# Norm chains of a decoder layer's front end rearranged, and the dense experts' partial sums carried through PSUM by ScalarE

## The chip, the cores and the metric

The kernel runs on one core of one Trainium2 chip. The metric is the device time of one launch in microseconds; each figure given as "the time" is the median of several runs.

## The reference, cut to what matters

One decoder layer on 1024 tokens of width 1024, all in f32. The parts that the change touches:

```python
h = rms_norm(x, norm1_gain) * (1 + scale1) + shift1
r_q, r_k, r_v, r_g, s_q, s_k, s_v = split(h @ w_in)            # 8 heads of 64 in each
y_ret = head_group_norm(retention(r_q, r_k, r_v)) * silu(r_g)  # mean and variance over 64
q_sb, k_sb = rms_norm(s_q, sb_q_gain), rms_norm(s_k, sb_k_gain)    # per head, over 64
z = q_sb @ k_sb.T / 8                                          # stick-breaking attention
log_beta = log_sigmoid(z)
...
x = x + gate1 * (concat(y_ret, rms_norm(y_sb)) @ w_out)
h2 = rms_norm(x, norm2_gain) * (1 + scale2) + shift2
# PEER: 8 heads, top 16 of 128 x 128 product keys, 16384 experts of one neuron each
a = gelu(h2 . expert_down[id]) * gate
x = x + gate2 * sum(a * expert_up[id])
```

## The kernel before

The 1024 tokens are eight tiles of 128. The attention part, which we call the front end, runs in three segments of 1, 3 and 4 tiles (`SEGS`). In each segment the seven projections are streams: eight 256 KB pieces of `w_in` come in, ScalarE and GpSimd split each piece into a high and a low half, and TensorE accumulates three products for each tile in an `acc` bank of PSUM. When a stream ends, an `ev_...` function evicts each tile's bank: `ev_rk`, `ev_rq`, `ev_rv`, `ev_rg` for retention, `ev_sk`, `ev_sq`, `ev_sv` for stick-breaking. The order of the last three streams and of the retention work between them is the string `RET` (h = `ret_head`, t = `ret_tail`).

Four norms form chains that cross engines. `head_norm` (L390, for `ev_sk` and `ev_sq`) squares the bank on ScalarE, sums over the head on VectorE, calls `rpow` (L79: scale and add epsilon on VectorE, power of -1/2 on GpSimd) and multiplies the bank by the result on VectorE (L396); then TensorE transposes the product (L327). `normed` (L299) does the same over the whole row before the transposes of L310. `ret_head` takes the mean off (L461, L463), squares, sums, calls `rpow` and multiplies (L470) before another transpose of L327. `sb_finish` (L542) takes sums of squares from TensorE in PSUM, adds epsilon on VectorE (L549), takes the power on GpSimd (L550), and copies on ScalarE before the transposes of L556. The stick-breaking weights are sigmoids of z and -z that ScalarE reads from PSUM (L514, L515); VectorE multiplies them up in a scan (L516).

The experts are computed in two ways. For tokens 0 to 511 (`gather_tile`) GpSimd issues one indirect DMA of 128 rows for each of 128 choices, once in `expert_down` and once in `expert_up`, for four tiles: 1024 gathers of 512 KB, each used up by one VectorE instruction (L780, L790). Four buffers `g` are in flight. Gathers 480 to 495 wait for the fifth piece of the dense part's routing (`HOLD`, `HOLD_C`), and all behind them on the queue with them. For tokens 512 to 1023 (`dense`) every expert is multiplied: stage 1 (L821 to L823) gives a block of 128 experts' activations, stage 2 (L924 to L926) adds the block's part to the output. Stage 2 goes in 32 groups of `GB` = 4 blocks; in each group it has eight output pieces of 128x512, numbered k. Pieces 0 and 1 stay in PSUM all the time (`held`). Pieces 2 to 7 take turns in the two other `acc` banks: twelve matmuls, and then VectorE adds the bank to `yacc` in SBUF (L937), or ScalarE copies it there in the first group (L935). In the last group (L930) VectorE multiplies by gate2 and adds.

The code is written in this order, the gathers last. The order of instructions on each engine is fixed at build time by the framework, which runs the program through a cost model and gives each engine the oldest piece of work that is ready (`schedule_with_timeline_sim`). So gathers lie between all the rest on VectorE's and GpSimd's queues, and each engine then keeps to that order on the chip.

Of the kernel before, what the change touches and what calls it, by code (L numbers as in the profile page):

```python
# [54 lines left out]
def tile_kernel(ctx, tc, A, out):  # L55
# [20 lines left out]
    def bcast_dram(ap, parts, n, off=0):  # L76
        return bass.AP(tensor=ap.tensor, offset=ap.offset + off, ap=[[0, parts], [1, n]])

    def rpow(o, in_, mul):  # L79
        DVE.tensor_scalar(o, in_, mul, EPS, op0=OP.mult, op1=OP.add)  # L80
        POOL.tensor_tensor(o, o, mhalf[:, 0:o.shape[-1]], op=OP.pow)


# [146 lines left out]
    def seg_gen(phase, t0, nt, hooks):  # L230
# [67 lines left out]

        def normed(x):  # L299
            st = small(1)  # L300
            ACT.activation(V((128, D), BF16), x, AF.Square, accum_out=st)
            rpow(st, st, 1.0 / D)
            ACT.activation(x, x, AF.Copy, scale=st)

        def to_T(xs, scale, shift):
# [11 lines left out]
        def hv(a):  # L317
            return a.rearrange("p (h d) -> p h d", d=64)
# [68 lines left out]
        stream(A["w_in"], 1536, hT_, ev_rg, False)  # L387


        def head_norm(acc, o):  # L390
            sq = V()
            ACT.activation(sq, acc, AF.Square)
            s = small(8)
            DVE.tensor_reduce(s, hv(sq), axis=AX.X, op=OP.add)
            rpow(s, s, 1.0 / 64)
            DVE.tensor_tensor(hv(o), hv(acc), s[:, :, None].to_broadcast([128, 8, 64]), op=OP.mult)  # L396

        def ev_sk(i, acc):
            t = t0 + i
            kn = V()  # L400
            head_norm(acc, kn)
            tp = transpose4(kn, anti)
            ACT.activation(kTr[:, :, 896 - 128 * t:1024 - 128 * t], q4(tp), AF.Copy, scale=gqk)

        qc = [U([128, 2, 512]) for i in range((nt + 1) // 2)]
        qT = [qc[i // 2][:, i % 2] for i in range(nt)]

        def ev_sq(i, acc):
            qn = V()
            head_norm(acc, qn)  # L410
            copy(qT[i], transpose4(qn, ident))

        def ev_sv(i, acc):
            v = V()
# [6 lines left out]
        def ret_head(i):  # L421
# [36 lines left out]
                                                     op0=OP.mult, op1=OP.add)  # L458
            mu = small(8)
            DVE.tensor_reduce(mu, hv(y), axis=AX.X, op=OP.add)  # L460
            DVE.tensor_scalar(mu, mu, 1.0 / 64, None, op0=OP.mult)  # L461
            yc = V()
            DVE.tensor_tensor(hv(yc), hv(y), mu[:, :, None].to_broadcast([128, 8, 64]), op=OP.subtract)  # L463
            sq = V()
            ACT.activation(sq, yc, AF.Square)
            va = small(8)
            DVE.tensor_reduce(va, hv(sq), axis=AX.X, op=OP.add)
            rpow(va, va, 1.0 / 64)
            DVE.tensor_mul(rg[i], rg[i], yc)
            DVE.tensor_tensor(hv(rg[i]), hv(rg[i]), va[:, :, None].to_broadcast([128, 8, 64]), op=OP.mult)  # L470

# [28 lines left out]
        def sb_weights(i, pr):  # L500
            t = t0 + i
            L = 128 * (t + 1)
            c0 = 896 - 128 * t
            w2 = []
            for hh in range(2):
                b = slice(64 * hh, 64 * hh + 64)
                be, sy = U([128, D]), U([128, D])
                for s0 in range(0, L, 512):
                    w = min(512, L - s0)
                    z = pstile("acc", 4)  # L510
                    PE.matmul(z[:, :w], q4(qT[i])[b, pr], kTr[b, pr, c0 + s0:c0 + s0 + w], start=True, stop=s0 > 0)
                    if s0 == 0:
                        PE.matmul(z[:, :128], ident, negm, start=False, stop=True)
                    ACT.activation(be[:, s0:s0 + w], z[:, :w], AF.Sigmoid)  # L514
                    ACT.activation(sy[:, s0:s0 + w], z[:, :w], AF.Sigmoid, scale=-1.0)  # L515
                DVE.tensor_tensor_scan(sy[:, :L], sy[:, :L], sy[:, :L], 1.0, op0=OP.mult, op1=OP.bypass)  # L516
                DVE.tensor_mul(be[:, 1:L], be[:, 1:L], sy[:, :L - 1])
                w2.append(be)
            return w2
# [22 lines left out]
        def sb_finish(i, yT):  # L542
# [3 lines left out]
            for pr in range(4):  # L546
                PE.matmul(tp[:, 2 * pr:2 * pr + 2], sq[:, pr], ones_bd[:, 0:128:64], start=True, stop=True)
            r = small(8)
            DVE.tensor_scalar(r, tp[:, 0:8], 1.0, EPS, op0=OP.mult, op1=OP.add)  # L549
            POOL.tensor_tensor(r, r, mhalf, op=OP.pow)  # L550
            tp = pstile("tp", 2)
            rx = V()
            copy(hv(rx), r[:, :, None].to_broadcast([128, 8, 64]))
# [246 lines left out]
    def dense(Hhi, Hlo, dp, kpg, late):  # L800
# [83 lines left out]
        for g0 in range(0, NB, GB):  # L884
# [28 lines left out]
            def stage2(k, bs):  # L913
                i, hf = divmod(k, 2)
                sl = slice(128 * i, 128 * i + 128)
                ds_ = slice(512 * hf, 512 * hf + 512)
                keep = k < len(held)
                if k not in ys:
                    ys[k] = held[k] if keep else pstile("acc", 4)
                y = ys[k]  # L920
                st, sp = not keep or g0 == 0, not keep or g0 + GB == NB
                for b in bs:
                    phi, plo, uhi, ulo = blk[b]
                    PE.matmul(y, phi[:, sl], uhi[:, ds_], start=st and b == 0, stop=False)  # L924
                    PE.matmul(y, phi[:, sl], ulo[:, ds_], start=False, stop=False)  # L925
                    PE.matmul(y, plo[:, sl], uhi[:, ds_], start=False, stop=sp and b == GB - 1)  # L926
                if b < GB - 1:
                    return
                ya = yacc[:, i, ds_]
                if g0 + GB == NB:  # L930
                    DVE.tensor_mul(ya, y, g2[:, ds_])
                    DVE.tensor_add(x1[i][:, ds_], x1[i][:, ds_], ya)
                    SP.dma_start(out[(NG + i) * 128:(NG + i + 1) * 128, ds_], x1[i][:, ds_])
                elif not keep and g0 == 0:
                    copy(yacc[:, i, ds_], y)  # L935
                elif not keep:
                    DVE.tensor_add(yacc[:, i, ds_], yacc[:, i, ds_], y)  # L937

            if g0 + GB == NB:

# [90 lines left out]
```

## Time and profile before

| what | value |
|---|---|
| runs | 3194.1, 3207.25, 3212.17 us, median 3207.25 us |
| profiled execution | 3201.63 us, its span 3199.8 us |
| TensorE matmul busy | 2693.4 us (84%) |
| VectorE busy | 2631.3 us (82%) |
| GpSimd busy | 1918.6 us (60%) |
| ScalarE busy | 1076.0 us (34%) |
| DMA | 899.19 MB, mean 281 GB/s |
| mean granted TensorE clock | 0.909 of full speed |

The shares are means over stages with different limits. The front end lies before about 1440 us, the dense part's routing between 1440 and 1840 us, the groups of stage 2 after 1840 us. PE is TensorE's matmuls, PEld its weight loads, DVE is VectorE, ACT ScalarE, POOL GpSimd, SP the queue of plain DMAs.

### The profile page before, as it was taken

The numbers are of one execution on the slowest core, as the hardware profiler recorded it, in microseconds if no ns is written. First come the engines' busy times: TensorE is split into PE (matmuls) and PEld (weight loads), VectorE is DVE, ScalarE is ACT, GpSimd is POOL, SyncE is SP. The second block draws the span as 40 slices with busy tenths as digits, with TensorE's granted clock in tenths as the row PEclk, the third lists the DMA queues.
The fourth block names the chain that finished last, engine by engine and source line by source line (L and its number), as shares of the span: only waits on it lengthen the run. The fifth ranks groups of instructions, "written<-read, shape, count | busy, mean of one in ns | idle before, by whom it ended". The sixth has DMA issues, their size and how long they took to land.

```text
span 3199.8 us, 38483 instructions
## 1 busy us (share of the span) xinstructions
PE 2693.4 (84%) x12308; PEld 2079.8 (65%) x12308; DVE 2631.3 (82%) x4913; ACT 1076.0 (34%) x1871; POOL 1918.6 (60%) x1542
## 2 busy tenths in 40 slices
PE   6867867777967678696878998869999999999997
PEld 2454654576755345575767787657887887888785
DVE  2269788789987899789999778999778877888888
ACT  1122224244321345332666632322232332222231
POOL 1025874677777567652478756556666666666664
PEclk9978886888978688897999999989999999999999
DMA  8688886898788766852368898788899999999897
GB/s 316 241 291 280 297 280 219 297 345 295 242 283 287 247 203 217 308 202 70 119 233 316 315 318 313 265 282 306 312 321 330 340 333 317 330 343 333 315 313 267
DMA packets 337642, 899.19 MB, mean 281 GB/s; under 512 B 38296, under 2 KB 105880, under 8 KB 333344
## 3 DMA queue, kind: packets, MB, share of 16 engines
q0 software_dynamic: 147456, 536.94, 48.3%
q1 hardware_dynamic: 189984, 359.80, 32.7%
q8 instruction: 97, 1.59, 0.2%
q14 instruction: 105, 0.86, 0.1%
HBM read 846.24 MB, written 50.35 MB: 280 GB/s over the span
## 4 chain that ended last, share of the span: by engine, by line
DVE 27%; PE 21%; DMA 21%; issue 15%; POOL 12%; ACT 2%; SPq 1%; POOLq 0%; DVEq 0%; ACTq 0%
DMA g<-in_up_dram,ids 10%; POOL g L769 8%; DVE g L780 5%; DMA g<-in_down_dram,ids 4%; DVE gy L790 4%; PE tp L821 2%; PE tp L822 2%; PE tp L823 2%; PE acc L263 2%; DMA rawu<-in_up_dram 2%; DVE p L860 2%; PE acc L924 2%; PE acc L926 2%; PE acc L925 2%; DVE dlo L812 1%
## 5 line engine op out<-in xcount | busy, mean ns | idle before, releaser
L769 POOL DMA_INDIRECT g<-in_up_dram,ids x512 | 594.8, 1162 | 404.7 <-DVE gy L790 281.2
L769 POOL DMA_INDIRECT g<-in_down_dram,ids x512 | 536.4, 1048 | 470.2 <-DVE g L780 275.9
L790 DVE SCALAR_TENSOR_TENSOR gy<-g,a,gy 128x1024 f32<-128x1024 f32 x508 | 651.3, 1282 | 148.2 <-DMA g<-in_up_dram,ids 144.8
L780 DVE SCALAR_TENSOR_TENSOR g<-g,gy 128x1024 f32<-128x1024 f32 x512 | 617.9, 1213 | 134.1 <-DMA g<-in_down_dram,ids 132.2
L924 PE MATMUL acc<-u,p 128*128 128x512 f32 x1024 | 402.2, 398 | 39.9 <-DVE yacc L937 20.4
L821 PE MATMUL tp<-Thi,dhi 128*128 128x512 f32 x1024 | 406.6, 397 | 30.0 <-ACT dhi L71 18.4
L926 PE MATMUL acc<-u,p 128*128 128x512 f32 x1024 | 386.6, 395 | 20.9 <-DVE p L906 20.9
L823 PE MATMUL tp<-Thi,dlo 128*128 128x512 f32 x1024 | 403.5, 394 | 0.5 <-POOL dlo L812 0.4
L822 PE MATMUL tp<-Tlo,dhi 128*128 128x512 f32 x1024 | 403.8, 394 | 0.0
L925 PE MATMUL acc<-u,p 128*128 128x512 f32 x1024 | 402.8, 395 | 0.0
L812 POOL TENSOR_TENSOR u<-rawu,u 128x1024 fp32r<-128x1024 f32 x128 | 306.4, 2403 | 32.0 <-ACT u L71 30.0
L271 POOL TENSOR_TENSOR wlo<-wraw,whi 128x512 fp32r<-128x512 f32 x182 | 236.8, 1307 | 95.4 <-ACT whi L71 64.8
L924 PEld LDWEIGHTS acc<-u,p 128*128 128x128 f32 x1024 | 194.9, 190 | 94.5 <-DVE yacc L937 27.4
L821 PEld LDWEIGHTS tp<-Thi,dhi 128*128 128x128 f32 x1024 | 195.3, 191 | 73.3 <-ACT dhi L71 19.4
L926 PEld LDWEIGHTS acc<-u,p 128*128 128x128 f32 x1024 | 194.7, 191 | 65.0 <-DVE p L906 24.4
L71 ACT ACTIVATE whi<-wraw 128x512 fp32r<-128x512 f32 x208 | 130.3, 630 | 311.8 <-DMA wraw<-in_w_in_dram 105.7
L71 ACT ACTIVATE u<-rawu 128x1024 fp32r<-128x1024 f32 x128 | 133.0, 1056 | 298.8 <-DMA rawu<-in_up_dram 195.5
L71 ACT ACTIVATE dhi<-rawd 128x1024 fp32r<-128x1024 f32 x128 | 135.4, 1058 | 278.0 <-PE tp L822 268.5
L280 PE MATMUL acc<-wlo,Thi 128*128 128x512 f32 x504 | 212.5, 422 | 16.1 <-POOL wlo L271 15.6
L823 PEld LDWEIGHTS tp<-Thi,dlo 128*128 128x128 f32 x1024 | 194.5, 190 | 41.6 <-POOL dlo L812 1.4
L925 PEld LDWEIGHTS acc<-u,p 128*128 128x128 f32 x1024 | 195.5, 191 | 40.0
L822 PEld LDWEIGHTS tp<-Tlo,dhi 128*128 128x128 f32 x1024 | 195.0, 190 | 39.5
(271 smaller groups left out, 4998.6 us busy)
## 6 DMA issues: line engine op xcount, KB each, us to landing
rawd<-in_downT_dram SPq DMA_DIRECT2D x128, 512.0 KB
rawu<-in_up_dram SPq DMA_DIRECT2D x128, 512.0 KB
gd<-u SPq DMA_DIRECT2D x32, 1024.0 KB
gm<-gd SPq DMA_DIRECT2D x512, 64.0 KB
wraw<-in_w_in_dram SPq DMA_DIRECT2D x112, 256.0 KB
u<-in_ada_w_dram SPq DMA_DIRECT2D x46, 512.0 KB
wraw<-in_wq_dram SPq DMA_DIRECT2D x64, 256.0 KB
u<-in_w_in_dram SPq DMA_DIRECT2D x28, 512.0 KB
```

The costliest lines, as they stand in the source:

```text
L71: ACT.activation(out_, in_, AF.Copy, scale=scale)
L271: (POOL if kt else DVE).tensor_sub(lo, raw, hi.bitcast(F32))
L769: POOL.indirect_dma_start(out=g, out_offset=None, in_=A[src], in_offset=bass.IndirectOffsetOnAxis(ap=groups[j // m][0][:, j % m:j % m + 1] ...
L780: DVE.scalar_tensor_tensor(g, g, 1.0, hp, op0=OP.mult, op1=OP.mult, accum_out=a[:, j:j + 1])
L790: DVE.scalar_tensor_tensor(y, g, a[:, j:j + 1], y, op0=OP.mult, op1=OP.add)
L812: eng.tensor_sub(lo, raw, hi.bitcast(F32))
L821: PE.matmul(a, dhi[:, sl], Hhi[:, kt], start=kt == 0, stop=False)
L822: PE.matmul(a, dhi[:, sl], Hlo[:, kt], start=False, stop=False)
L823: PE.matmul(a, dlo[:, sl], Hhi[:, kt], start=False, stop=kt == KT - 1)
L924: PE.matmul(y, phi[:, sl], uhi[:, ds_], start=st and b == 0, stop=False)
L925: PE.matmul(y, phi[:, sl], ulo[:, ds_], start=False, stop=False)
L926: PE.matmul(y, plo[:, sl], uhi[:, ds_], start=False, stop=sp and b == GB - 1)
```

## The change

In the front end `rpow` loses its scale: the squares are scaled in ScalarE's own instruction, and epsilon is added on GpSimd. `ev_sk` and `ev_sq` first copy the bank to SBUF on ScalarE. `ev_sk` then normalises the copy. `ev_sq` transposes the copy as it is; the heads' factors go to a small tile `qs` (factor and its negative) that the two sigmoids take as a scale. In `ret_head` the division of the mean goes into the subtraction. `sb_finish` copies the sums out of PSUM on ScalarE.

In stage 2, for pieces 2 to 7 of groups 1 to 30, ScalarE copies `yacc` into the new bank before the first matmul, no matmul restarts the sum, and ScalarE copies the bank back to `yacc` after the last; VectorE's addition is gone.

```diff
-    def rpow(o, in_, mul):
-        DVE.tensor_scalar(o, in_, mul, EPS, op0=OP.mult, op1=OP.add)
+    def rpow(o, in_):
+        POOL.tensor_scalar(o, in_, EPS, None, op0=OP.add)
         POOL.tensor_tensor(o, o, mhalf[:, 0:o.shape[-1]], op=OP.pow)
...
-            ACT.activation(V((128, D), BF16), x, AF.Square, accum_out=st)
-            rpow(st, st, 1.0 / D)
+            ACT.activation(V((128, D), BF16), x, AF.Square, scale=1.0 / 32, accum_out=st)
+            rpow(st, st)
...
-        def head_norm(acc, o):
+        def head_scale(x, s):
             sq = V()
-            ACT.activation(sq, acc, AF.Square)
-            s = small(8)
+            ACT.activation(sq, x, AF.Square, scale=0.125)
             DVE.tensor_reduce(s, hv(sq), axis=AX.X, op=OP.add)
-            rpow(s, s, 1.0 / 64)
-            DVE.tensor_tensor(hv(o), hv(acc), s[:, :, None].to_broadcast([128, 8, 64]), op=OP.mult)
+            rpow(s, s)
         def ev_sk(i, acc):
             t = t0 + i
             kn = V()
-            head_norm(acc, kn)
+            copy(kn, acc)
+            s = small(8)
+            head_scale(kn, s)
+            DVE.tensor_tensor(hv(kn), hv(kn), s[:, :, None].to_broadcast([128, 8, 64]), op=OP.mult)
...
         def ev_sq(i, acc):
-            qn = V()
-            head_norm(acc, qn)
-            copy(qT[i], transpose4(qn, ident))
+            q = V()
+            copy(q, acc)
+            copy(qT[i], transpose4(q, ident))
+            head_scale(q, qs[i][:, 0])
+            DVE.tensor_scalar(qs[i][:, 1], qs[i][:, 0], -1.0, None, op0=OP.mult)
...
-            DVE.tensor_scalar(mu, mu, 1.0 / 64, None, op0=OP.mult)
             yc = V()
-            DVE.tensor_tensor(hv(yc), hv(y), mu[:, :, None].to_broadcast([128, 8, 64]), op=OP.subtract)
-            sq = V()
-            ACT.activation(sq, yc, AF.Square)
+            DVE.scalar_tensor_tensor(hv(yc), mu[:, :, None].to_broadcast([128, 8, 64]), -1.0 / 64, hv(y),
+                                     op0=OP.mult, op1=OP.add)
             va = small(8)
-            DVE.tensor_reduce(va, hv(sq), axis=AX.X, op=OP.add)
-            rpow(va, va, 1.0 / 64)
+            head_scale(yc, va)
...
-                    ACT.activation(be[:, s0:s0 + w], z[:, :w], AF.Sigmoid)
-                    ACT.activation(sy[:, s0:s0 + w], z[:, :w], AF.Sigmoid, scale=-1.0)
+                    h = 2 * pr + hh
+                    ACT.activation(be[:, s0:s0 + w], z[:, :w], AF.Sigmoid, scale=qs[i][:, 0, h:h + 1])
+                    ACT.activation(sy[:, s0:s0 + w], z[:, :w], AF.Sigmoid, scale=qs[i][:, 1, h:h + 1])
...
-            DVE.tensor_scalar(r, tp[:, 0:8], 1.0, EPS, op0=OP.mult, op1=OP.add)
-            POOL.tensor_tensor(r, r, mhalf, op=OP.pow)
+            copy(r, tp[:, 0:8])
+            rpow(r, r)
...
+                back = not keep and 0 < g0 < NB - GB
                 if k not in ys:
                     ys[k] = held[k] if keep else pstile("acc", 4)
+                    if back:
+                        copy(ys[k], yacc[:, i, ds_])
                 y = ys[k]
-                st, sp = not keep or g0 == 0, not keep or g0 + GB == NB
+                st, sp = not back and (not keep or g0 == 0), not keep or g0 + GB == NB
...
-                elif not keep and g0 == 0:
+                elif not keep:
                     copy(yacc[:, i, ds_], y)
-                elif not keep:
-                    DVE.tensor_add(yacc[:, i, ds_], yacc[:, i, ds_], y)
```

## Rows read from the trace of the kernel before

**Rows 1.** Windows: busy us of PE, PEld, DVE, ACT, POOL, clock, DMA share, GB/s

```profile
0.00:1440.00 1440.00, 1093.10 (x4979) 763.06 (x4980) 1131.42 (x2378) 468.62 (x894) 841.27 (x731) 0.84 0.79 269
...
1920.00:2160.00 240.00, 197.17 (x799) 155.77 (x798) 228.07 (x510) 65.69 (x84) 142.36 (x103) 0.90 0.84 286
2160.00:3184.00 1024.00, 1002.55 (x4370) 821.09 (x4368) 842.39 (x1028) 280.17 (x363) 652.09 (x488) 1.00 0.92 322
```

**Rows 2.** Windows of line 769, the gathers' issue on POOL

```profile
0.00:1440.00 1440.00, 537.55 (x480) 0.84 0.79 269
1440.00:1600.00 160.00, 0.00 (x0) 0.86 0.26 95
...
1920.00:3184.00 1264.00, 509.64 (x472) 0.98 0.90 315
```

**Rows 3.** Timeline from 3180 us: PE's last matmul, DVE's last gather product

```profile
3183.69 0.39 PE L926 MATMUL acc<-u,p 128*128 128x512 f32 x1
...
3190.64 1.29 DVE L790 SCALAR_TENSOR_TENSOR gy<-g,a,gy 128x1024 f32<-128x1024 f32 x1 [1.62 <-DMA g<-in_up_dram,ids]
```

**Rows 4.** Waits of PE in 0:1440: total us, times, longest

```profile
PE tp L327 <- DVE v L396: 77.4, 15, 17.0
PE tp L310 <- ACT u L303: 55.2, 15, 13.1
PE tp L556 <- ACT v L71: 39.0, 6, 10.4
PE tp L327 <- DVE u L470: 26.8, 2, 19.2
```

**Rows 5.** Timeline of PE: gaps before transposes, ident for Q, anti for K

```profile
103.83 1.08 PE L327 MATMUL tp<-ident,v 128*128 128x128 f32 x4 [3.39 <-DVE v L396]
...
448.92 1.09 PE L327 MATMUL tp<-ident,v 128*128 128x128 f32 x4 [17.00 <-DVE v L396]
...
927.79 2.04 PE L327 MATMUL tp<-anti,v 128*128 128x128 f32 x8 [14.46 <-DVE v L396]
...
990.99 1.11 PE L327 MATMUL tp<-ident,v 128*128 128x128 f32 x4 [12.02 <-DVE v L396]
...
1014.20 0.63 PE L327 MATMUL tp<-ident,v 128*128 128x128 f32 x4 [2.60 <-DVE v L396]
```

**Rows 6.** Timeline of DVE before the gap that ends at 990.99

```profile
983.23 0.16 DVE L80 TENSOR_SCALAR s<-s 128x8 f32<-128x8 f32 x1
983.30 1.22 DVE L780 SCALAR_TENSOR_TENSOR g<-g,gy 128x1024 f32<-128x1024 f32 x1
```

**Rows 7.** Groups by line and form: busy us, mean ns, then idle before

```profile
L81 POOL TENSOR_TENSOR s<-s,mhalf 128x8 f32<-128x8 f32 x24 | 40.1, 1671 | 47.3 <-DVE s L80 46.9
L71 ACT ACTIVATE gy<-g 128x1024 f32<-128x1024 f32 x4 | 4.1, 1024 | 1.3 <-DMA g<-h2d 1.3
L469 DVE TENSOR_TENSOR u<-u,v 128x512 f32<-128x512 f32 x8 | 6.8, 846 | 0.0
```

**Rows 8.** Groups of single tiles and lines: ns minimum/median/maximum, starts

```profile
L937 DVE TENSOR_TENSOR yacc<-yacc,acc x180: 661/681/692, 1912.9 to 3148.1; 128x512 f32<-128x512 f32 x180
L71 ACT ACTIVATE yacc<-acc x6: 592/598/598, 1872.2 to 1890.8; 128x512 f32<-128x512 f32 x6
L470 DVE TENSOR_TENSOR u<-u,s x8: 675/688/691, 89.7 to 1090.8; 128x512 f32<-128x512 f32 x8
```

**Rows 9.** Waits of PE in 1840:3184

```profile
PE acc L926 <- DVE p L906: 20.9, 7, 6.1
PE acc L924 <- DVE yacc L937: 20.4, 8, 5.4
PE acc L924 <- ACT p L71: 17.4, 13, 3.5
```

**Rows 10.** Waits of ACT in 1920:3184

```profile
ACT u L71 <- DMA rawu<-in_up_dram: 189.7, 49, 14.6
ACT p L71 <- DVE tp L903: 181.9, 55, 6.8
```

More of the change, by code (lines that the diff above doesn't have):

```diff
@@ L406, in seg_gen @@
         qT = [qc[i // 2][:, i % 2] for i in range(nt)]
+        qs = [vp.tile([128, 2, 8], F32, name="qs", bufs=4) for i in range(nt)]
         def ev_sq(i, acc):
-            qn = V()
-            head_norm(acc, qn)
-            copy(qT[i], transpose4(qn, ident))
+            q = V()
[3 more added lines that the diff above has]
+            DVE.tensor_scalar(qs[i][:, 1], qs[i][:, 0], -1.0, None, op0=OP.mult)
         def ev_sv(i, acc):
@@ L917, in stage2 @@
                 keep = k < len(held)
+                back = not keep and 0 < g0 < NB - GB
                 if k not in ys:
                     ys[k] = held[k] if keep else pstile("acc", 4)
+                    if back:
+                        copy(ys[k], yacc[:, i, ds_])
                 y = ys[k]
-                st, sp = not keep or g0 == 0, not keep or g0 + GB == NB
+                st, sp = not back and (not keep or g0 == 0), not keep or g0 + GB == NB
                 for b in bs:
                     phi, plo, uhi, ulo = blk[b]
-                    PE.matmul(y, phi[:, sl], uhi[:, ds_], start=st and b == 0, stop=False)
-                    PE.matmul(y, phi[:, sl], ulo[:, ds_], start=False, stop=False)
-                    PE.matmul(y, plo[:, sl], uhi[:, ds_], start=False, stop=sp and b == GB - 1)
+                    PE.matmul(y, phi[:, sl], uhi[:, ds_], start=st and b == 0, stop=False, skip_group_check=True)
+                    PE.matmul(y, phi[:, sl], ulo[:, ds_], start=False, stop=False, skip_group_check=True)
+                    PE.matmul(y, plo[:, sl], uhi[:, ds_], start=False, stop=sp and b == GB - 1, skip_group_check=True)
                 if b < GB - 1:
```

## The prediction

> **What bounds the kernel now.** I read the windows first, to part the stages, then in each stage what PE waits for, then the queues of the engines it waits for.
>
> The windows show two different kernels [rows 1]. Up to 1440 us no engine is full: PE is busy 1093 of 1440 us at a mean clock of 0.84, VectorE 1131, ScalarE 469, and the DMA engines 0.79 of the time. From 2160 us on PE is busy 1002.6 of 1024 us at full clock; that stage is bound by PE, with DMA close behind at 0.92. Between them, at 1920 to 2160, VectorE is busy 228 of 240 us and PE only 197: there the late routing of the gathered tokens loads VectorE.
>
> The gathers run beside all of this. 480 of them are issued by 1440 us, none from 1440 to 1600 us, since the next ones are held for the dense part's routing, and 472 in the last 1264 us, 2.68 us each [rows 2]. So the gathers have about 200 us in hand at the end of the front end, and a shorter front end moves the hold, and all behind it, forward by as much. At the end both halves finish together: PE's last matmul starts at 3183.7 us and VectorE's last gather product at 3190.6 us [rows 3]. To end earlier, both must.
>
> In the front end PE's largest waits are for the four norm chains: 77.4 us for L396 (Q and K), 55.2 us for `normed`, 39.0 us for `sb_finish`, 26.8 us for `ret_head` [rows 4], together 198 of PE's 347 idle us. In the dense part PE's waits are few: 20.4 us for the additions to be removed, 20.9 us for VectorE's low halves `plo`, 17.4 us for ScalarE's high halves `phi` [rows 9].
>
> **The change in the front end.** *Q.* Six gaps before a Q transpose make 42.5 us (3.39, 17.00, 12.02, 2.99, 4.49 and 2.60); the first, the two longest and the last stand in [rows 5]. The chain behind them is long because VectorE's short steps queue among gather products: a 0.16 us step is followed by one of 1.22 us [rows 6]. After the change a Q transpose waits for one ScalarE copy out of PSUM, 0.6 us by the same form [rows 8]. With handing over and ScalarE's queue I put 1.5 us on each of eight tiles: 42.5 - 12 is about 30 us saved. Bounds: 42.5 us, and nothing if PE only waits elsewhere. The chain itself goes on beside it and is wanted by the first sigmoid; the V stream (96 matmuls in the last segment) and the retention work lie between, longer than the 12 us it now costs. What comes late next on PE is the `ret_head` transpose.
>
> *K.* The other 77.4 - 42.5 = 35 us are K's. Its chain gets a ScalarE copy (0.6 us) longer and loses one VectorE place; the bank comes free after the copy, not after the product, so matmuls of the next stream may go first. Bounds: 35 us saved if they fill the gap, 8 x 1.5 = 12 us lost if not. I take 0, since the gap of 14.46 us [rows 5] is one chain long and the chain stays.
>
> *The other chains.* `normed`, `sb_finish` and `ret_head` each lose one VectorE place, `ret_head` two. A place is the step and one gather product before it, 0.16 + 1.22 = 1.4 us [rows 6]. About 15 such places end at a PE gap (5 of `normed`, 6 of `sb_finish`, 2 x 2 of `ret_head`): 21 us. GpSimd's added addition of 128x8 is in no row; it costs between nothing and the 1.67 us of the power of the same size [rows 7]. I take 0.5 us, since an addition is less than a power and both wait in one queue: -7 us. The `sb_finish` gaps lie beside VectorE's scans, which bound that stretch, so I count 10 us of the 14.
>
> The Trainium skill speaks against this step: "GPSIMD Engine Reference", section 3 on performance versus the Vector engine, keeps elementwise work on VectorE and gives a ratio of 1.96 for an addition. By that ratio, an estimate from the 0.16 us step, the addition would take 0.3 us, and the 15 places 5 us instead of 7.
>
> *At nothing:* the mean's division (8 x 0.16 us on VectorE), the 16 ScalarE copies and the scale operand of 192 sigmoids; ScalarE is busy 469 of 1440 us [rows 1]. Without that cover they would cost some 20 us. K's product now reads two SBUF operands; the nearest row, `ret_head`'s product from SBUF, takes 675 to 691 ns [rows 8], as the one from PSUM did.
>
> The Trainium skill's "SBUF — State Buffer", section "Who interferes with whom", has a VectorE instruction with two SBUF inputs contend with GpSimd instructions that read SBUF. The full-width product of L469 (846 ns mean, [rows 7]) may show that, the broadcast one of L470 doesn't; by the rule K's eight products would cost 1.3 us more. The removed additions have one PSUM input, so by it GpSimd gains nothing from their going.
>
> Front end together: 30 + 0 + 10 = 40 us saved. No DMA and nothing on SP's queue is added or moved.
>
> **The change in the dense part.** VectorE loses 180 x 0.681 = 123 us. ScalarE gains 180 copies out (0.598 us, [rows 8]) and 180 copies in; for a copy from SBUF to PSUM the row is 1.02 us at twice the width [rows 7], so 0.5 to 0.6 us. Together some 210 us over 1264, on an engine busy 346 there: 44%, not full.
>
> A bank's turnaround grows: before, one addition of 0.68 us; after, a copy out and a copy in, 1.2 us, before the next piece's first matmul. If all of the extra 0.5 us showed on PE, 180 x 0.5 = 92 us; if PE has matmuls of the other bank or of stage 1 to do, nothing. What decides is ScalarE's order. It waits 189.7 us for `rawu` from DMA (up to 14.6 us at a time) and 181.9 us for VectorE [rows 10]; a copy behind such a wait holds PE. The nearest row is PE's wait for `phi`, which stands in the same queue: 17.4 us [rows 9] for 128 copies, 0.14 us each, so 180 turnarounds cost about 25 us. Against it stand the 20.4 us of waits for L937 that go, and some of the 20.9 us for `plo`, which VectorE makes sooner. PE's idle time in 1920 to 3184 us is only 64 us in all (197.2 + 1002.6 busy of 1264, [rows 1]), so more can't be gained there. I take 0 for the sum, with bounds of -60 and +92.
>
> What freed VectorE time does start is gathers; at a DMA share of 0.92 they can gain only a few per cent, and need no more, since they only have to keep up with PE.
>
> **The sum.** The profiled execution took 3201.6 us; 3201.6 - 40 + 0 = 3161.6 us. The median of the runs is 5.6 us above it, so 3167 us.
>
> **The rivals.**
>
> *The dense part gains too.* VectorE's load of 228 in 240 us falls by its share of the 123 us, 23 us, PE's waits for it and what follows from it go, and the gathers keep up: two thirds of the 62 us of waits in [rows 9], 40 us more, 3127 us. For it: VectorE is full there. Against it: ScalarE waits for the same VectorE.
>
> *ScalarE holds PE (the slower side).* Its in-order waits for `rawu` and for VectorE fall before the copies in or out, and the turnaround's 0.5 us shows each time: 92 us, against 40 gained, 3259 us. It decides from 40/180 = 0.22 us for each turnaround. For it: the waits of [rows 10], longer than any slack of two banks. Against it: before, VectorE too waits for its gathers, and its additions held PE for 20.4 us only.
>
> *The front end gets no shorter.* The gaps only move to the next chain, since VectorE is busy 1131 of 1440 us and gathers fill what it gets free; dense part even: 3207 us. For it: the next chain, `ret_head`, is a 19.2 us gap right behind Q's. Against it: the Q gaps hold nothing on VectorE but gathers and other tiles' steps.
>
> **How the numbers follow.** The forecast has 0.52, its own range 3140 to 3190 (10 to 65 us saved); the dense gain 0.15; ScalarE's hold 0.18; no shorter front end 0.15. About 0.5%, 16 us, is what a measurement of this kernel can tell from no change. Faster: nearly all of the first, the second, a little of the last, 0.66. Same: most of the last and a weak form of the hold, 0.17. Slower: 0.17. The range goes from 3115, past the dense gain's 3127, to 3230, where the hold shows a little over 0.3 us for each turnaround; its full form lies outside.
>
> **What would show it.** Right: the gaps of 17.0 and 12.0 us before Q transposes fall under 2 us; the dense stage's first matmuls come about 40 us earlier; PE's wait at L924 for the copies in stays near 25 us, and PE stays 97% busy from then on. Wrong: PE waits at L924 for `acc` from ScalarE of over 65 us; or the K gaps grow; or the stage from 1920 us loses its idle time altogether.

## The result and the profile after

The changed kernel takes 3160.0 us (median of 3159.1, 3161.0, 3181.8 and 3140.8 us) against 3208.2 us (3194.1 to 3212.2 us, four runs), a ratio of 0.9874 with a 95% interval of 0.984 to 0.9908. It is faster by 1.3%, or 40 us. (The quotient of the two medians is 0.985, or 48 us; it lies in the interval as well.) The forecast was 3167 us, from a range of 3140 to 3190. The profiled execution took 3159.1 us with a span of 3157.3 us, 42.5 us under that of before, where the sum said 40.

The windows of the changed kernel, with the columns of [rows 1], show that both halves moved:

```profile
0.00:1440.00 1440.00, 1115.46 (x5128) 787.62 (x5128) 1146.26 (x2458) 504.79 (x935) 864.29 (x784) 0.86 0.80 271
...
1920.00:2160.00 240.00, 219.54 (x924) 176.74 (x923) 218.91 (x532) 116.41 (x174) 146.37 (x106) 0.96 0.88 303
2160.00:3140.00 980.00, 951.37 (x4130) 780.86 (x4129) 744.23 (x800) 410.80 (x610) 636.71 (x476) 0.99 0.92 325
```

PE is 97% busy in the last stretch (951.4 of 980 us), ScalarE 42% (before 27%), VectorE 76% (before 82%). At 1920 to 2160 us PE has 22 us more work in the same time than in [rows 1].

The waits of PE in the front end (0 to 1290 us: total us, times, longest), which answer to [rows 4]:

```profile
PE tp L310 <- ACT u L303: 48.4, 14, 12.3
PE tp L561 <- ACT v L71: 21.4, 7, 5.0
PE tp L327 <- DVE u L474: 20.6, 2, 16.3
...
PE tp L535 <- DVE u L522: 15.8, 7, 4.2
PE tp L446 <- DVE v L442: 13.2, 4, 10.1
...
PE tp L327 <- DVE v L403: 6.6, 5, 2.2
...
PE tp L327 <- ACT v L71: 1.8, 2, 1.1
```

`head_norm`'s 77.4 us have become 6.6 us for K (L403) and 1.8 us for Q's copy. `sb_finish` (now L561) fell from 39.0 to 21.4 us, `normed` from 55.2 to 48.4, `ret_head` (now L474) from 26.8 to 20.6. That makes 99.6 us of waits less, where the prediction counted 40. Some of it only moved: the waits at L535 and L446 were 0.9 and 4.7 us before (L530, L439). Up to the last score matmul (place A below) PE's idle time as a whole falls by 67 us, from 317.6 of 1268 to 250.8 of 1186 us. In PE's timeline the gaps before the transposes, which answer to [rows 5], are these (start, us, then the gap and its releaser):

```profile
906.92 1.13 PE L327 MATMUL tp<-anti,v 128*128 128x128 f32 x8 [2.16 <-DVE v L403]
...
922.17 1.13 PE L327 MATMUL tp<-anti,v 128*128 128x128 f32 x8 [1.45 <-DVE v L403]
...
940.70 1.12 PE L327 MATMUL tp<-ident,v 128*128 128x128 f32 x4 [0.69 <-ACT v L71]
...
1018.95 1.08 PE L327 MATMUL tp<-ident,u 128*128 128x128 f32 x4 [16.35 <-DVE u L474]
```

Q's gaps are under 2 us, K's anti-diagonal gap of 14.46 us is 2.16 us, and `ret_head`'s is the long one that stays.

So much for the front end; the end of the kernel moved far less than these waits. The waits of PE between the last transpose of the second norm and the first matmul of the dense part's stage 1 show where it went, first in the changed kernel (1299 to 1483 us), then in the kernel before (1368 to 1502 us):

```profile
PE tp L826 <- ACT dhi L71: 45.0, 1, 45.0
PE tp L641 <- ACT v L71: 34.8, 4, 11.0
```

```profile
PE tp L821 <- ACT dhi L71: 18.2, 1, 18.2
PE tp L636 <- ACT v L71: 16.8, 6, 4.4
```

L641 (before: L636) transposes the keys' scores for the top-k; L826 (before: L821) is the first instruction of stage 1, and in the changed kernel it comes 45 us after PE's last work. Together the two waits have grown by 45 us. The operand of L826 is a plain copy of loaded data. In ScalarE's timeline that copy stands behind a small step of the top-k that waits for VectorE:

```profile
1481.53 0.23 ACT L742 ACTIVATE ge<-ge 128x32 f32<-128x32 f32 x1 [9.07 <-DVE ge L741]
1481.66 1.04 ACT L71 ACTIVATE dhi<-rawd 128x1024 fp32r<-128x1024 f32 x1
```

The bound of this stretch is VectorE, busy all of 1400 to 1480 us, with PE at 6.2 and 0.0 us of each 40 us and a granted clock of 0.55 and 0.50 (columns of [rows 1]):

```profile
1400.00:1440.00 40.00, 6.23 (x24) 5.35 (x24) 40.00 (x146) 4.21 (x7) 16.57 (x19) 0.55 0.75 233
1440.00:1480.00 40.00, 0.00 (x0) 0.00 (x0) 40.00 (x255) 2.97 (x6) 0.37 (x1) 0.50 0.12 37
```

What VectorE does there besides the top-k are gather products (L795, before: L790; 1.28 us each). Windows of that line on VectorE, from the second norm's last transpose to the first stage-1 matmul, in the changed kernel and in the kernel before:

```profile
1299.10:1482.80 183.70, 75.44 (x59) 0.78 0.66 221
```

```profile
1368.30:1501.90 133.60, 20.49 (x16) 0.89 0.39 137
```

The stretch is 50.1 us longer now and holds 55 us more of them.

In the dense part the waits of PE from 1840 to 3150 us answer to [rows 9]:

```profile
PE acc L932 <- ACT p L71: 32.0, 14, 7.1
PE acc L934 <- DVE p L911: 6.1, 3, 3.7
PE acc L932 <- ACT acc L71: 6.0, 6, 2.3
PE acc L932 <- DVE yacc L939: 4.8, 1, 4.8
```

The 20.4 us for the additions are gone, the low halves fell from 20.9 to 6.1 us, the high halves rose from 17.4 to 32.0 us, and the copies into the banks cost 6.0 us where the prediction had 25. The copies themselves, which answer to [rows 8] (ns minimum/median/maximum, first and last start):

```profile
L71 ACT ACTIVATE yacc<-acc x186: 573/600/605, 1850.2 to 3107.9; 128x512 f32<-128x512 f32 x186
L71 ACT ACTIVATE acc<-yacc x180: 577/602/617, 1867.8 to 3100.6; 128x512 f32<-128x512 f32 x180
```

In the waits of ScalarE from 1920 to 3140 us, the rows of [rows 10] are 168.1 us for `rawu` and 136.5 us for VectorE; a new row of 203.7 us is its wait for a bank to be finished. The high halves come behind that wait on ScalarE's queue; whether it is what makes PE's wait for them longer was not tried.

### The profile page after: what moved, and what is told of

Its sections match the earlier page's. It is cut to its first block, busy times and chain, and to the rows that moved or that the text cites. A ratio compares the mean times of both kernels' runs of the same rounds, so it can differ in the third digit from the quotient of the medians.

```text
span 3157.3 us, 38775 instructions
## 1 busy us (share of the span) xinstructions
PE 2680.1 (85%) x12308; PEld 2078.8 (66%) x12308; DVE 2539.2 (80%) x4677; ACT 1297.0 (41%) x2254; POOL 1938.5 (61%) x1590
## 4 chain that ended last, share of the span: by engine, by line
DVE 24%; DMA 23%; PE 18%; issue 17%; POOL 14%; ACT 3%; SPq 1%; POOLq 0%; DVEq 0%; ACTq 0%
DMA g<-in_up_dram,ids 10%; POOL g L774 9%; DVE g L785 4%; DMA g<-in_down_dram,ids 4%; DVE gy L795 4%; DMA rawu<-in_up_dram 3%; PE acc L263 2%; DMA gm<-gd 2%; POOL u L817 2%; PE tp L826 2%; PE tp L827 2%; PE tp L828 2%; DVE dlo L817 1%; DVE p L865 1%; PE acc L932 1%
## 5 line engine op out<-in xcount | busy, mean ns | idle before, releaser
L774 POOL DMA_INDIRECT g<-in_down_dram,ids x512 | 582.5, 1138 | 461.9 <-DVE g L785 283.9
L795 DVE SCALAR_TENSOR_TENSOR gy<-g,a,gy 128x1024 f32<-128x1024 f32 x508 | 651.7, 1283 | 169.8 <-DMA g<-in_up_dram,ids 165.3
L774 POOL DMA_INDIRECT g<-in_up_dram,ids x512 | 552.2, 1078 | 364.5 <-DVE gy L795 197.4
L826 PE MATMUL tp<-Thi,dhi 128*128 128x512 f32 x1024 | 405.2, 396 | 48.6 <-ACT dhi L71 45.3
L271 POOL TENSOR_TENSOR wlo<-wraw,whi 128x512 fp32r<-128x512 f32 x182 | 236.0, 1304 | 61.6 <-ACT whi L71 33.9
L817 DVE TENSOR_TENSOR dlo<-rawd,dhi 128x1024 fp32r<-128x1024 f32 x122 | 209.2, 1715 | 57.5 <-ACT dhi L71 54.6
L826 PEld LDWEIGHTS tp<-Thi,dhi 128*128 128x128 f32 x1024 | 194.4, 190 | 91.2 <-ACT dhi L71 46.3
```

Source lines behind the costliest of these rows:

```text
L271: (POOL if kt else DVE).tensor_sub(lo, raw, hi.bitcast(F32))
L774: POOL.indirect_dma_start(out=g, out_offset=None, in_=A[src], in_offset=bass.IndirectOffsetOnAxis(ap=groups[j // m][0][:, j % m:j % m + 1] ...
L795: DVE.scalar_tensor_tensor(y, g, a[:, j:j + 1], y, op0=OP.mult, op1=OP.add)
L817: eng.tensor_sub(lo, raw, hi.bitcast(F32))
L826: PE.matmul(a, dhi[:, sl], Hhi[:, kt], start=kt == 0, stop=False)
```

## The experiments

After the result we held this theory: the chains' rearrangement shortens the front end by twice the forecast, more than half of it is given back in the routing stretch because the gathers up to the hold now fall among the top-k, and the kernel's end is the later of two halves, PE's stage 2 and the gathers. The rivals: the saving comes from VectorE's relief in the dense part; the front end's saving is small and the routing stretch is as long as it must be; ScalarE's longer turnaround (a bank's copy out and the next copy in, before PE goes on) costs PE time that another gain hides. The table gives the places that the following sections speak of. A is the start of the last scan-stage score matmul, B the last transpose of the second `normed`, C the first matmul of stage 1, with the number of gather products on VectorE between B and C; then the start of PE's first and last stage-2 matmul of the first form, the first gather issued after the hold and the last one, and the mean time of one between these two (in us). Each row is one profiled execution, the runs of one kernel lie 13 to 41 us apart, and each kernel gets an order of instructions of its own when it is built; so a few us between two rows decide nothing.

| kernel | A | B | C - B (products) | stage 2 from | PE last | gathers resume | last | each | ratio of times, 95% |
|---|---|---|---|---|---|---|---|---|---|
| before | 1268 | 1368 | 133.6 (16) | 1862 | 3183 | 1629.5 | 3182.7 | 2.86 | 1 |
| after | 1186 | 1299 | 183.7 (59) | 1839 | 3145 | 1610.2 | 3139.2 | 2.82 | 0.9874, 0.9840-0.9908 |
| e1 front end only | 1181 | 1295 | 185.7 (59) | 1840 | 3151 | 1610.4 | 3157.5 | 2.85 | 0.9911, 0.9888-0.9934 |
| e2 dense part only | 1257 | 1360 | 134.9 (16) | 1859 | 3179 | 1622.0 | 3170.5 | 2.85 | 0.9983, 0.9964-1.0002 |
| e3 Q only | 1231 | 1335 | 152.2 (33) | 1852 | 3170 | 1614.8 | 3182.6 | 2.89 | 0.9982, 0.9963-1.0002 |
| e4 after, hold 448 | 1179 | 1294 | 144.1 (27) | 1799 | 3114 | 1564.1 | 3167.9 | 2.79 | 0.9959, 0.9935-0.9983 |
| e5 after without Q | 1241 | 1347 | 160.9 (42) | 1868 | 3176 | 1637.6 | 3171.4 | 2.82 | 0.9910, 0.9874-0.9945 |
| e6 K only | 1242 | 1348 | 145.6 (26) | 1855 | 3163 | 1620.6 | 3176.0 | 2.86 | 0.9990, 0.9971-1.0010 |
| e7 copies in twice | 1181 | 1296 | 183.7 (59) | 1836 | 3151 | 1607.6 | 3140.2 | 2.82 | 0.9877, 0.9847-0.9907 |
| e8 after, hold 448, 5 buffers | 1198 | 1301 | 124.6 (0) | 1796 | 3127 | 1555.8 | 3073.0 | 2.64 | 0.9785, 0.9759-0.9811 |
| e9 before, 5 buffers | 1268 | 1371 | 124.6 (0) | 1867 | 3196 | 1625.2 | 3072.9 | 2.67 | 0.9985, 0.9964-1.0006 |
| e10 Q only, 5 buffers | 1233 | 1336 | 125.6 (8) | 1832 | 3177 | 1591.7 | 3052.9 | 2.69 | 0.9917, 0.9888-0.9947 |
| e11 after, 5 buffers | 1201 | 1307 | 137.8 (25) | 1821 | 3146 | 1577.2 | 3007.6 | 2.63 | 0.9832, 0.9802-0.9862 |
| e12 after, hold 416, 5 buffers | 1210 | 1295 | 124.8 (0) | 1797 | 3112 | 1551.6 | 3131.3 | 2.60 | 0.9803, 0.9769-0.9837 |

**The two halves, e1 and e2.** e1 is the changed kernel with stage 2 as it was:

```diff
-                    if back:
-                        copy(ys[k], yacc[:, i, ds_])
...
+                elif not keep and g0 == 0:
+                    copy(yacc[:, i, ds_], y)
                 elif not keep:
-                    copy(yacc[:, i, ds_], y)
+                    DVE.tensor_add(yacc[:, i, ds_], yacc[:, i, ds_], y)
```

> Only the front end of the change; stage 2 adds on VectorE as before. Theory 1 (given back): the chains bring PE about 75 us forward up to the second normed, and VectorE's top-k stretch, which must also take the gathers up to the hold, gives about 50 of it back; stage 2 starts about 20 us earlier and the time falls by 20 to 25 us, ratio 0.993. Theory 2 (the prediction's terms): 40 us faster, ratio 0.9875. Theory 3 (all of the gain is the front end's): 48 us faster, ratio 0.985.

e2 is the kernel before with the change's stage 2, the same edit the other way round.

> Only stage 2 of the change; the front end as before. Theory 1: VectorE's waits ahead of PE fall in the stretch from 1920 to 2160 us and ScalarE's copies hold PE for little; 20 to 25 us faster, ratio 0.993, nearly all of it between 1920 and 2160 us. Theory 2 (the prediction's terms): 0, ratio 1.000. Theory 3: 0 or slightly slower.

Measured: e1 3174.3 us, 0.9911, clearly faster; e2 3196.8 us, 0.9983 with 1 in its interval. For e1 the interval holds Theory 1's 0.993 and neither of the other two; for e2 it holds 1.000 and not 0.993. The front end has most of the gain (28 us, of 40 by the ratios or 48 by the medians), the dense part alone at most 0.4% (12 us). In e2 the first three waits of PE from 1840 to 3180 us are:

```profile
PE acc L927 <- ACT p L71: 36.5, 15, 8.3
PE acc L929 <- DVE p L906: 10.2, 5, 4.6
PE acc L927 <- ACT acc L71: 6.2, 5, 3.2
```

The same exchange as in the whole change: the waits for the additions go, those for the high halves grow. PE's stage 2, from first to last start, takes 1320.7 us against 1321.6 before. So the first rival falls. The 1305.9 us of the whole change are no clear sign for it either: with stage 2 as before, e1, e3 and e6 take 1310.9, 1318.0 and 1308.0 us. From e1 to the whole change PE ends 6 us earlier and the gathers 18 us earlier, all of these 18 by their pace (2.85 to 2.82 us, with the same start); from before to e2 the pace gains 0.01 us only. What VectorE's relief is worth to the gathers is therefore not settled by these single profiles.

**Parts of the front end, e3, e6 and e5.** e3 is before with the late scaling of Q alone:

```diff
-            qn = V()
-            head_norm(acc, qn)
-            copy(qT[i], transpose4(qn, ident))
+            q = V()
+            copy(q, acc)
+            copy(qT[i], transpose4(q, ident))
+            sq = V()
+            ACT.activation(sq, q, AF.Square)
+            DVE.tensor_reduce(qs[i][:, 0], hv(sq), axis=AX.X, op=OP.add)
+            rpow(qs[i][:, 0], qs[i][:, 0], 1.0 / 64)
+            DVE.tensor_scalar(qs[i][:, 1], qs[i][:, 0], -1.0, None, op0=OP.mult)
...
-                    ACT.activation(be[:, s0:s0 + w], z[:, :w], AF.Sigmoid)
+                    ACT.activation(be[:, s0:s0 + w], z[:, :w], AF.Sigmoid, scale=qs[i][:, 0, h:h + 1])
...
```

> Only the late scaling of Q: bank copied and transposed at once, the factors taken by the sigmoids; all else as before. By the prediction's terms 30 us faster (0.9906) and the Q gaps of 17.0 and 12.0 us under 2 us. If the gain is given back in the top-k stretch: the scans end about 35 us earlier, but stage 2 starts 10 to 20 us earlier and the time falls by as much (0.995).

e6 is before with K's copy alone, and the norm then taken from the copy:

```diff
-            head_norm(acc, kn)
+            copy(kn, acc)
+            head_norm(kn, kn)
```

> The kernel before with one addition: K's bank is copied to SBUF on ScalarE first and the norm works on the copy, so the bank comes free early. Prediction's term: 0 (K's gaps of 14.5, 5.7 and 3.3 us stay, the time within 5 us). If the early bank lets the next stream's matmuls go ahead of K's transposes: these gaps fall under 3 us each and the scans end 20 to 30 us earlier; the time falls by 5 to 10 us, ratio 0.997, since part is given back.

e5 is the changed kernel with Q normalised before its transposes again, by the new `head_scale`, and with constant scales in the sigmoids:

```diff
+            s = small(8)
+            head_scale(q, s)
+            DVE.tensor_tensor(hv(q), hv(q), s[:, :, None].to_broadcast([128, 8, 64]), op=OP.mult)
             copy(qT[i], transpose4(q, ident))
-            head_scale(q, qs[i][:, 0])
...
```

> The changed kernel, but Q is normalised before its transposes as K is (copy, square, sum, GpSimd, product), and the sigmoids take plain numbers. Prediction's terms (Q is 30 of the 40 us): 30 us slower than the changed kernel, ratio to before 0.997. If Q's gain is mostly given back behind the front end, as the run of Q alone says: the scans end 30 to 40 us later than in the changed kernel, stage 2 starts 10 us later, and the time is 5 to 12 us more, ratio 0.990.

The groups of L327 by form in e3 and then in e6 (busy us, mean ns, then the idle time ahead and what ended it; ident with `v` is Q and the transposes of another line, anti is K):

```profile
L327 PE MATMUL tp<-ident,v 128*128 128x128 f32 x96 | 16.2, 300 | 23.4 <-DVE v L352 17.9 <-ACT v L71 4.2 <-DVE ii L738 0.7
L327 PE MATMUL tp<-anti,v 128*128 128x128 f32 x64 | 13.9, 386 | 32.2 <-DVE v L396 32.2
```

```profile
L327 PE MATMUL tp<-ident,v 128*128 128x128 f32 x96 | 18.7, 333 | 66.6 <-DVE v L396 48.5 <-DVE v L352 18.1
L327 PE MATMUL tp<-anti,v 128*128 128x128 f32 x64 | 10.2, 313 | 3.2 <-DVE v L396 3.2
```

Each edit takes out its own gaps and leaves the other's. By these groups the 77.4 us of before are 45.0 us for Q and 32.4 us for K (the prediction's reading of the timeline had 42.5 and 35; it left out two gaps of 0.22 and 2.33 us before Q's transposes at 454 and 462 us). Q's are 4.2 us in e3, K's 3.2 us in e6, from a copy that makes the chain longer. The bank is free after the copy, so the next stream's matmuls go on while the chain runs; this was the upper bound of the prediction's K term. Place A comes 37 us earlier by Q alone and 26 us by K alone. The times do not show it: 0.9982 and 0.9990, both with 1 in the interval, and e3's interval lies above both expected ratios (0.9906 and 0.995). In e3 PE ends 13 us earlier and the gathers not at all; in e6 PE 20 us and the gathers 7 us. e5 gives 0.9910 against the whole change's 0.9874; the intervals overlap, so Q's worth inside the whole, some 11 us by the ratios, is not resolved. In e5 place A comes 55 us later than in the changed kernel and stage 2 29 us later, more than the 30 to 40 and 10 us expected.

**The hold, e4.** The changed kernel with 32 gathers fewer ahead of the routing:

```diff
-HOLD, HOLD_C = 480, 4
+HOLD, HOLD_C = 448, 4
```

> The changed kernel with the gathers held from number 448 on, 32 earlier than before (480). If the gathers' 1.28 us products on VectorE are what gives the front end's gain back, 32 fewer of them before the hold let the top-k stretch end about 40 us earlier and stage 2 start 40 us earlier, and if the gathers then keep up, the time falls by up to 40 us against the changed kernel (3120 us, ratio to before 0.973). Rival: the top-k stretch is bound by its own VectorE work and the weights, and stage 2 starts within 10 us of the changed kernel's 1850. Second rival: stage 2 starts earlier, but 32 more gathers at 2.6 us each, 83 us, end last: same time as the changed kernel or up to 45 us slower.

The stretch from B to C falls from 183.7 to 144.1 us and its gather products from 59 to 27; stage 2 starts 40 us earlier, and PE ends 30 us earlier. But the kernel takes 3185.5 us, 0.9959: slower than the changed kernel, as the second rival had it. The window of the products from B to C and the gathers' row in e4:

```profile
1294.00:1438.10 144.10, 34.48 (x27) 0.84 0.48 166
```

```profile
L774 POOL DMA_INDIRECT g<-in_up_dram,ids x512: 932/940/2571, 517.2 to 3167.9; - x171
```

576 gathers are left after the hold instead of 544, and at 2.79 us each they end 54 us after PE's last matmul begins. This shows two things: the 50 us were given back to gathers among the top-k, and PE alone does not set the end.

**The turnaround, e7.** The changed kernel with each copy into a bank made twice, 180 copies of 0.6 us more on ScalarE:

```diff
                     if back:
                         copy(ys[k], yacc[:, i, ds_])
+                        copy(ys[k], yacc[:, i, ds_])
```

> The changed kernel with ScalarE's copy of yacc into the bank done twice over, 180 more copies of 0.6 us on the bank's turnaround. If the turnaround has slack: TensorE's wait for the copies in stays under 10 us and the time is that of the changed kernel within 8 us. By the prediction's price of 0.14 us for each: 25 us slower. If ScalarE's order holds TensorE: 100 us slower.

3163.3 us, 0.9877: the same as the changed kernel. The wait in question, in e7 from 1840 to 3150 us:

```profile
PE acc L933 <- ACT acc L71: 9.5, 6, 5.5
```

It rose by 3.5 us in all, for 108 us more of work. The banks' turnaround has room for nearly all of another 0.6 us, so the rival in which ScalarE holds PE falls with its mechanism.

**The gathers out of the way, e9, e10 and e11.** Five buffers `g` for gathers instead of four, paid for with one buffer fewer in each of two other pools (`up` of the front end; `p2` of the routing and the dense part, which holds the high and low halves), in the kernel before (e9), in Q only (e10) and in the changed kernel (e11):

```diff
-            g = gp.tile([128, D], F32, name="g", bufs=4)
+            g = gp.tile([128, D], F32, name="g", bufs=5)
...
-            return dp.tile(shape, dt, name="p2", tag="p2", bufs=11)
+            return dp.tile(shape, dt, name="p2", tag="p2", bufs=10)
...
-            with tc.tile_pool(name="wp", bufs=1) as wp, tc.tile_pool(name="up", bufs=13) as up, \
+            with tc.tile_pool(name="wp", bufs=1) as wp, tc.tile_pool(name="up", bufs=12) as up, \
```

> The kernel before with five buffers for the gathers (one less each in the front end's large tiles and in the dense part's), hold at 480 as before; the base for the next run. If the four buffers made the gathers end last: they end 40 us or more ahead of TensorE, TensorE's last matmul stays near 3184 us, and the time is 3185 to 3200 us, 5 to 15 us less than before.

> The late scaling of Q alone, with five buffers for the gathers. Theory: Q alone brought TensorE's last matmul 14 us forward, and the gathers, which still ended last, hid it; with them out of the way the time is 10 to 15 us below that of five buffers alone. Rival: Q's gain is lost in VectorE's top-k stretch whatever the gathers do; within 5 us of five buffers alone.

> The changed kernel with five buffers for the gathers, hold at 480 as before. If the hold is what brought the version with 448 forward (stage 2 from 1839 to 1796 us), this one starts stage 2 near 1840 us and takes 3150 to 3165 us, that of the changed kernel or 10 us less; if the buffers did it, 3135 us.

The gathers' row in e9 and the row of PE's first stage-2 form in e9, then the same of PE in e10:

```profile
L769 POOL DMA_INDIRECT g<-in_up_dram,ids x512: 935/948/3808, 501.1 to 3072.9; - x171
```

```profile
L926 PE MATMUL acc<-u,p x1024: 387/389/796, 1869.4 to 3196.8; 128*128 128x512 f32 x171
```

```profile
L932 PE MATMUL acc<-u,p x1024: 387/389/796, 1832.0 to 3176.8; 128*128 128x512 f32 x171
```

In e9 the gathers end 110 us earlier than before, 123 us ahead of PE, and the time stays (3202.9 us, 0.9985; the 5 to 15 us expected are not resolved): PE's half alone keeps it there. In e10 on the same footing Q brings 26 us by the medians (3202.9 to 3176.7 us) and 22 by the ratios (0.9985 to 0.9917, intervals apart), more than the 10 to 15 us expected, while with four buffers it brought nothing that can be resolved. So Q is worth something near the prediction's 30 us where the gathers allow it, and with four buffers the gathers hid it in two ways: they took 19 us of it among the top-k (133.6 to 152.2 us from B to C; 124.6 to 125.6 with five buffers), and they still ended last. From e9 to e11 the whole change is worth 55 us by the medians, 49 by the ratios. e11 lies between its two expectations: the buffers alone start stage 2 at 1821 us, and the time is 3147.6 us.

The fifth buffer has its price. In each of the four pairs that differ by it PE's stage 2 takes longer: 1329.8 against 1321.6 us (e9, before), 1344.8 against 1318.0 (e10, e3), 1325.1 against 1305.9 (e11, after), 1330.6 against 1315.0 (e8, e4). Whether the fifth buffer's traffic, the smaller `p2` or the smaller `up` causes that was not tried.

**Both together, e8 and e12.** e8 is e11 with the hold at 448, e12 with the hold at 416.

> The changed kernel with the gathers held from 448 on and five buffers for them in place of four (one buffer less each in the front end's large tiles and in the dense part's). If the four buffers set the gathers' pace of 2.65 us: it falls to about 2.3 us, TensorE's last matmul comes near 3115 us as with the hold at 448 alone, and the time is 3125 to 3140 us, below both kernels. If bandwidth sets it: pace within 3%, gathers end last near 3170 us, time 3175 to 3195 us.

> The changed kernel with five buffers for the gathers and the hold at 416. 32 gathers fewer before the hold, 41 us of VectorE's products: if the top-k stretch still carries that many, stage 2 starts 30 to 40 us before 1796 us, TensorE ends near 3095 us, and the gathers, 80 us later than 3073, end last: 3150 us or so. If gathers no longer lie in the top-k stretch at 448, stage 2 starts at 1796 as well and only the gathers' end moves: 3155 to 3170 us.

e8 takes 3135.1 us, 0.9785 (0.9759 to 0.9811), and beats both kernels: no gather product lies between B and C, the stretch is 124.6 us long, stage 2 starts at 1796 us, and the gathers end 53 us before PE. Their pace is 2.64 us, against 2.79 in e4; it was expected to fall from 2.65 to 2.3, and the smaller gain was enough. In e12 the stretch is no shorter (124.8 us), the later gathers are more, and they end last again: 3142.9 us, below the expected 3150 to 3170 and not distinguishable from e8. PE's waits in e8 from 1795 to 3130 us say what is next:

```profile
PE acc L932 <- ACT p L71: 59.8, 10, 11.1
PE acc L932 <- ACT acc L71: 5.7, 7, 1.7
```

## Why the prediction was right, point by point

**What bounds the kernel.** That both halves must end earlier was right, and by it the outcomes of e3, e4 and e6 can be read. Wrong was the step "the gathers have about 200 us in hand at the end of the front end". The pause seen in [rows 2] was counted as slack; but a front end that is 69 us shorter (place B) also leaves less time for the 480 gathers, and 43 more products fall into a stretch where VectorE is the bound. The fourteen kernels give one curve: the stretch is 124.6 to 124.8 us long with no product, 125.6 with 8, 133.6 to 134.9 with 16, 137.8 to 145.6 with 25 to 27, 152.2 with 33, 160.9 with 42 and 183.7 to 185.7 with 59, each product taking 1.28 us of VectorE. The first 8 cost 1 us and the first 16 some 10, and from 16 to 59 the stretch grows by 1.17 us for each.

**Q, 30 us.** The gaps fell as forecast (45.0 us by the groups, 42.5 in the prediction, to 1.8 us). Q alone brings A forward by 37 us, and 22 to 26 us of time where the gathers allow it (e10).

**K, 0.** Mis-sized: its gaps went from 32.4 us (35 in the prediction) to 6.6 us, and in e6 alone place A comes 26 us earlier. The prediction named the reason (the bank comes free after the copy) as its bound of 35 and chose the chain's length instead. The runs are near the bound.

**The other chains, 10 us.** Their waits fell by 6.8 us (`normed`), 17.6 us (`sb_finish`) and 6.2 us (`ret_head`), 30.6 us together. The gaps of `sb_finish`, discounted for VectorE's scans, gave the most. No run took these chains one by one, so what they are worth in time is not shown. GpSimd's added addition was taken at 0.5 us; it is 0.26:

```profile
L80 POOL TENSOR_SCALAR s<-s 128x8 f32<-128x8 f32 x24 | 6.3, 264 | 88.0 <-ACT s L71 44.4 <-DVE s L394 42.5
```

By the ratio of the Trainium skill's "GPSIMD Engine Reference", section 3, our estimate was 0.3 us. The trace has less, a median of 241 ns for L80's steps on GpSimd against 163 ns on VectorE before, 1.48 times; the page's 1.96 is for two inputs of 2048 elements. Whether its advice to keep such steps on VectorE pays here is not shown, since no run moved epsilon alone; a VectorE place stood behind a gather product of 1.22 us [rows 6].

**Front end together, 40 us.** Place A came 82 us earlier. Up to A PE is busy 935.2 of 1186 us at a mean clock of 0.86 for the same 4269 matmuls that took 950.4 of 1268 us at 0.83. So 67 us are waits and 15 us busy time at the higher clock, and the clock was in no term of the sum. The two windows (columns of [rows 1]), before and after:

```profile
0.00:1268.00 1268.00, 950.38 (x4269) 648.91 (x4270) 990.44 (x2014) 404.13 (x787) 733.12 (x637) 0.83 0.80 272
```

```profile
0.00:1186.00 1186.00, 935.23 (x4269) 643.83 (x4270) 927.52 (x1902) 426.55 (x807) 700.40 (x632) 0.86 0.80 269
```

Of the 82 us 13 were lost by B and 50 between B and C; stage 2 starts 23 us earlier. The forecast of "about 40 us earlier" for its first matmuls was off by 17 us, in a sum of two errors of opposite sign.

**At nothing.** The sigmoids' scale operand costs 93 ns each at 128x512 (696 against 603 ns):

```profile
L519 ACT ACTIVATE u<-acc,qs 128x512 f32<-128x512 f32 x48 | 33.4, 696 | 33.1 <-PE acc L517 29.3 <-PE acc L515 3.6
...
L403 DVE TENSOR_TENSOR v<-v,s 128x512 f32<-128x512 f32 x8 | 5.6, 699 | 2.2 <-POOL s L81 2.1
```

192 of them, the narrower ones counted alike, are some 18 us of ScalarE at most, in a stretch where it is busy 505 of 1440 us. K's product from SBUF (L403) takes 699 ns, 8 ns above the range in [rows 8]; none of the eight started while GpSimd was at its split of a weight piece (L271, a subtraction of two SBUF tiles). Where such a product starts with 0.4 us or more of L271 still to go, it takes longer: eight of them, in e5, e6, e8, e11 and e12, took 0.97 to 1.79 us. From PSUM it stays at 0.69 us beside the same line. Here are e5 and then the kernel before:

```profile
924.85 1.28 POOL L271 TENSOR_TENSOR wlo<-wraw,whi 128x512 fp32r<-128x512 f32 x1
924.90 1.79 DVE L403 TENSOR_TENSOR v<-v,s 128x512 f32<-128x512 f32 x1 [0.20 <-POOL s L81]
```

```profile
390.99 1.25 POOL L271 TENSOR_TENSOR wlo<-wraw,whi 128x512 fp32r<-128x512 f32 x1
391.03 0.69 DVE L396 TENSOR_TENSOR v<-acc,s 128x512 f32<-128x512 f32 x1 [1.03 <-POOL s L81]
```

So the rule that the prediction took from the Trainium skill's "SBUF — State Buffer", section "Who interferes with whom", is not seen in the changed kernel's row, and these traces agree with it. A broadcast second operand counts too, which the prediction, from L470, took as doubtful. It cost up to 1.1 us at a time, too little to bear on the result.

**The dense part, 0.** Right for PE: e2 is within 0.4% of before, and PE's stage 2 alone is 1 us shorter in it. Two terms inside were off and made up for each other: the copies in cost 6.0 us instead of 25, and the high halves, which share ScalarE's queue, cost 14.6 us more. In the whole change PE's stage 2 is 15.7 us shorter (1305.9 against 1321.6 us), of which e1, with VectorE's additions still there, has 10.7; e6, with K's copy alone, has 13.6. So most of this gain comes without the dense edit, and what makes stage 2 shorter in these kernels stays open.

**The rivals.** ScalarE's hold is ruled out by e7. The dense gain did not show as a gain of PE; e2 bounds it at 12 us. (Its 62 us of waits count 3.4 us of L821 that [rows 9] does not show; the three rows make 58.7.) "The front end gets no shorter, since gathers fill what it gets free" described most of what happened between B and C, and fell short because 23 us got through.

**The sum.** 40 us were forecast and 42.5 measured in the profiled execution; the ends moved by 38.4 us (PE) and 43.5 us (gathers). Of the gathers' 43.5 us, 19.3 come from the earlier release after the hold and 24 from the pace, 2.82 instead of 2.86 us. That the total agrees is partly luck. PE's 38 us are 82 us at A (67 of waits, 15 of clock), less 13 up to B and 50 from there to C, plus 4 up to stage 2 and 16 from a stage 2 that runs shorter (each rounded). The sum had 40 in one piece, and neither the clock, the loss nor the shorter stage 2.

## What to carry to other kernels

Where two independent halves end together, follow both through the change: a gain on one shows only up to the end of the other, and a part that measures as nothing (Q at 0.9982) can be worth over 20 us once the other half is out of the way. A fixed hold or hand-written order is tuned to the length of what stands before it, so when that gets shorter, ask first which work now slides into the next bound stretch. And a copy that frees a PSUM bank early can be worth more than the step it adds to the chain behind it.

## What the runs showed of the hardware that was not expected

The gathers' pace follows the number of buffers even where the DMA engines look full: 2.79 to 2.89 us each with four buffers in nine kernels, 2.60 to 2.69 us with five buffers in five kernels, at a DMA share of 0.91 and 0.93 (1840 to 3000 us, after and e11) and 321 against 334 GB/s. From after to e11 that is 7%, where the prediction read a share of 0.92 as leaving a few per cent. Two other pools had a buffer less in these five, so the fifth gather buffer is the likely cause, not one tried alone. The faster gathers came with a stage 2 that was 8 to 27 us longer.

The waits went along with a lower clock: the mean granted clock up to place A rose from 0.83 to 0.86 when PE's gaps went, and it stood at 0.50, the lower of its two levels (1.2 GHz), in the 40 us without a matmul before stage 1 (1440 to 1480 us, after).

A copy of 128x512 on ScalarE takes the same from SBUF into PSUM (602 ns) as from PSUM into SBUF (600 ns).

A product on VectorE that reads both operands from SBUF took 0.97 to 1.79 us instead of 0.69 when GpSimd was in the middle of subtracting two SBUF tiles (e5, e6, e8, e11, e12). Where the product had started first, GpSimd's subtraction took 1.61 to 1.68 us instead of 1.3 (after, e4, e7). The same product from PSUM did not change (0.69 us, before).
